# Column maxima spread by a product with the repeated column as weights; the engines of the vector steps chosen anew

## The chip, the core and the metric

The kernel runs on one core of one Trainium2 chip. A core has five engines with a queue each: TensorE (PE in the profile; its weight loads are PEld), VectorE (DVE), ScalarE (ACT), GpSimd (POOL) and SyncE (SP), which here issues every DMA. Each engine works through its own queue in order; an instruction whose input is not ready holds back all that is queued behind it. Engines wait for each other by semaphores. The metric is device microseconds (us) of one execution, lower is better.

## What is computed

One step of a hybrid attention encoder, for 1024 prompt rows with 16 meta rows ahead of them, and for 32 sample rows that attend to a cache of 272 rows:

```python
h = rmsnorm(x) * g
dq, dk, dv, fq, fk, fv, fl, gate = split(h @ w_in)      # 1024 x 4104
# 4 differential heads: two softmax maps each, subtracted
ad = softmax(q1 k1' - alibi) - lam * softmax(q2 k2' - alibi);  od = rmsnorm(ad @ dv) * subln_g * 0.2
# 8 forgetting heads: softmax with a bias from cumulative log-sigmoid gates
of = softmax(fq fk' + F_q - F_k) @ fv
y = rmsnorm(x + (concat(od, of) * silu(gate)) @ w_out) * final_norm_g
# the outputs: y, and the new rows of k, v and log f
```

All inputs and outputs are float32. To reach that accuracy with 16-bit products, each operand is split into a high and a low half (`hi = fp16(s*x)`, `lo = fp16(s*x - hi)`), and each product is made of three.

## The kernel before

Nothing in the code is in the order in which the engines run it. Functions describe tasks (`add(engine, cost, function, priority, deps, buffers taken, buffers used)`), and `Graph.order` simulates the engines with the costs given there (ns) and writes out the order: whenever an engine is idle in that simulation, the ready task with the lowest priority number gets it, if its buffers are free. The instructions are then issued in that order, so that a task with a wrong cost shifts what follows on its engine.

The main parts are these.
- `x_tasks` (lines 512 to 603): nine tiles of x are normalised and split into `hT`, the transposed input. Three tiles are transposed by PE, six by DMA. `XO` is the order of the tiles, `XG` the engine that multiplies by g ("d" DVE, "p" POOL), for the tiles that go by DMA.
- `w_tasks` (from line 654): a block of 128 columns of w_in is loaded, ACT sums the absolute values of each row (L668), `scale_tasks` turns the row sums into one scale for the whole block, and the block is split into hi and lo. The two halves are made by ACT and DVE (L687, L689), by POOL and DVE (`W_POOL`, L683), or by POOL, ACT and POOL (`W_FULL`, L674, L676, L678).
- `spread_task` (L615 to L627) brings a column of 128 values, one per partition, to all partitions: POOL makes a diagonal matrix of it (L623), PE multiplies it by a matrix of ones (L627), DVE takes the maximum over the row (L640 in `scale_tasks`, L799 in `v_tasks`). It is called 51 times: for each of the 32 blocks of w_in, the forget weights, the 8 blocks of v, w_out, and 9 tiles of the output.
- `proj_tasks`: the 32 projections (L869), their transposes and, for the gates, the chain exp, ln, exp on ACT, one product on POOL or DVE (`GATE_POOL`, L973), and two on DVE (L977, L978), which frees the accumulator.
- `unit_tasks`: 128 rows against their keys (block i has 144 + 128 i keys). Scores on PE (L1273), bias and minimum on DVE (L1287), exp on ACT (L1293), reciprocal on DVE (L1297 to L1301). For pairs 0 to 3 (differential) the second map is scaled on POOL (L1305), combined on DVE (L1317), split by ACT (L1322) and by POOL or DVE (`DIFF_POOL`, L1328). For pairs 4 to 7 (forgetting) the split is ACT and DVE (L1336, L1344), POOL and DVE (`FOX_POOL`, L1339, L1344), or POOL scale, ACT copy, POOL subtraction (`FOX_FULL`, L1350, L1355, L1361). A DMA transposes the result, and PE multiplies by v (L1385 to L1392).
- `out_tasks`: w_out is loaded, summed (L1681), scaled and split (`WO_FULL`: POOL, ACT, POOL at L1701 to L1705; `WO_POOL`: POOL L1712 and DVE L1716; else ACT L1714 and DVE L1716) into `hT`, which must be free by then. Nine output tiles: load, product with the gate (L1751), sum (L1765), spread, split (L1768, L1770), 48 products each (L1798), final norm.
- A warm-up of 24 float32 products of the identity (L1856) runs at the start.

Of the kernel before, what the change touches and what calls it, by code (L numbers as in the profile page):

```python
# [59 lines left out]
WO_POOL = (4, 7)  # L60
W_FULL = {"v": (1, 2, 4, 5, 7), "k": (0,), "q": (6,)}
FOX_FULL = (2, 3, 6)
AHEAD = 400.0
# [4 lines left out]
WARM = 24  # L68

# [193 lines left out]
def tile_hymba(  # L263
# [17 lines left out]
             "Q0": 2, "Q1": 2, "Q2": 2, "kq": 2, "diag": 2, "ge": 2, "G": 2, "kr": 1, "vr": 1, "vs": 1, "ksh": 1, "ksl": 1, "sP": 1,  # L281
# [78 lines left out]
    onesb = T([128, 128], BF16, "onesb")  # L360
# [28 lines left out]
    def consts():  # L389
# [4 lines left out]
        def f2():  # L394
# [12 lines left out]
            pool.tensor_copy(out=identb, in_=ident)  # L407
# [207 lines left out]
    def spread_task(col_, prio, deps):  # L615


        dh, th = Hold("diag"), Hold("tr")
        loc = {}

        def fd():
            loc["d"] = T([128, 128], BF16, "diag", RINGS["diag"])
            pool.tensor_scalar(out=loc["d"], in0=ident, scalar1=col_, scalar2=1.0, op0=ALU.mult, op1=ALU.mult)  # L623

        def f():
            loc["t"] = PSUM("tr")[:, 0:128]
            mm(loc["t"], onesb, loc["d"], start=True, stop=True)  # L627
        td = add("pool", 370 + PORT_P, fd, prio, list(deps) + [cn["id"]], [dh])
        return loc, th, add("pe", 60, f, prio, [td, cn["one"]], [th], [dh])

    def scale_tasks(parts, prio, deps, outs):


        m, sc = stat(), stat()
        if parts.shape[-1] > 1:
            deps = [add("dve", 150, lambda: dve.tensor_reduce(out=m, in_=parts, axis=AX.X, op=ALU.max), prio, deps)]
        loc, th, t1 = spread_task(m if parts.shape[-1] > 1 else parts, prio, deps)
# [13 lines left out]
    def w_tasks(key, prio):  # L651
# [6 lines left out]
        a, u = stat(), stat()  # L658
# [115 lines left out]
    def v_tasks(p, prio):  # L774
# [10 lines left out]
        a, b, mx, sc, u = (stat() for _ in range(5))  # L785
# [236 lines left out]
    def forget_tasks(prio):  # L1022
# [7 lines left out]
        wa, wu = stat(), stat()  # L1030
# [213 lines left out]
    def unit_tasks(p, hd, gg, prio, bias, av):  # L1244
# [5 lines left out]
        for bi in range(2):  # L1250
# [6 lines left out]
            for m in maps:  # L1257
# [38 lines left out]
                def fq(r=r, rk=rk, sm=sm, m=m):  # L1296
# [3 lines left out]
                    elif m == 0:  # L1300
                        dve.tensor_scalar(out=rk, in0=r, scalar1=lam3[1], scalar2=None, op0=ALU.mult)  # L1301
                t = add("dve", 300 + 0.4 * PORT, fq, prio + 0.3, [te, cn["lam"]])
                if p < 4 and m == 1:
                    def fp(ph=ph, nk=nk, r=r):
                        pool.tensor_scalar(out=A(ph, nk), in0=A(ph, nk), scalar1=r, scalar2=lam3[2],  # L1305
                                           op0=ALU.mult, op1=ALU.mult)
                    t = add("pool", c_ts(nk), fp, prio + 0.3, [t], [], [ph])
# [5 lines left out]
            on_pool = i in (DIFF_POOL if p < 4 else FOX_POOL)  # L1313
# [17 lines left out]
            else:  # L1331
# [15 lines left out]
                full = i in FOX_FULL  # L1347
                if full:
                    def fp(ph=P[m], nk=nk, r=rec[m][1]):
                        pool.tensor_scalar(out=A(ph, nk), in0=A(ph, nk), scalar1=r, scalar2=2.0 ** 15, op0=ALU.mult,  # L1350
                                           op1=ALU.mult)
# [11 lines left out]
                    t = add("pool", c_ts(nk), fp, prio + 0.2, [t], [], [P[m]])  # L1363
# [268 lines left out]
    def out_tasks(prio, early_q):  # L1632
# [88 lines left out]
        for t, (c0, n, j) in enumerate([(1024, 32, 8)] + [(128 * j, 128, j) for j in range(8)]):  # L1721
# [33 lines left out]
            a, u = stat(), stat()  # L1755
# [186 lines left out]
```

## Time and profile before

| | us |
|---|---|
| median of 3 runs | 774.92 |
| lowest, highest | 774.81, 775.51 |
| the profiled execution | 774.65 |
| its span, first to last instruction | 772.7 |
| mean granted TensorE clock (share of full) | 0.946 |
| busy: PE, DVE, ACT, POOL | 675.7, 601.3, 506.1, 394.4 |
| instructions | 14780 |

The profiled execution took 1.95 us more than its span, and 0.27 us less than the median. Busy time of PE is the union of its products' records; products overlap each other in time, so the row of one product is longer than its share. A row of the trace gives start and length of an instruction, or of several merged ones (x8), in us; a line number stands for the line of the kernel that issued it; `out<-in` are the names of tiles.

### The profile page before, as it was taken

Reading aid. Unit: us, or ns where it says so; the run is one execution under the profiler, and the core shown is the slowest. Engines: PE = TensorE matmul, PEld = TensorE weight load, DVE = VectorE, ACT = ScalarE, POOL = GpSimd, SP = SyncE. Lnnn points to the kernel's source line nnn. Section 1 sums busy time; section 2 is a strip of 40 time slices with the busy share of each in tenths; the row PEclk is TensorE's granted clock in tenths of the full one; section 3 lists DMA queues with packets and bytes.
Section 4 is the critical chain, followed back from the end, with each engine's and each line's share of the span. In section 5 each row is a group of like instructions: output and inputs, shape, how many; then the busy total and the mean of one; then the engine's idle time right before and its main releaser. Section 6 shows DMA issues by size and latency. Waiting matters only on the chain. (4 is left out here: it accounts for less than half of the span.)

```text
span 772.7 us, 14780 instructions
## 1 busy us (share of the span) xinstructions
PE 675.7 (87%) x4967; PEld 450.5 (58%) x4967; DVE 601.3 (78%) x1631; ACT 506.1 (66%) x1156; POOL 394.4 (51%) x542
## 2 busy tenths in 40 slices
PE   5379787998999799899799989898999984599996
PEld 5256455666666566576576667666756653234443
DVE  5975888877888588888878987886887888847643
ACT  5654666576677496687777688777679787434332
POOL 0556562586577477876748375562642455510000
PEclk8579999999999899999999999999999997599998
DMA  8376543667453565567577996795599788948411
GB/s 235 79 168 116 120 109 51 93 131 113 71 134 89 109 139 111 119 146 135 133 112 151 162 208 147 152 190 153 113 223 221 164 195 231 262 136 244 145 55 55
DMA packets 236444, 110.48 MB, mean 143 GB/s; under 512 B 150112, under 2 KB 228264, under 8 KB 236368
## 3 DMA queue, kind: packets, MB, share of 16 engines
q1 hardware_dynamic: 236368, 109.54, 65.6%
q8 instruction: 39, 0.64, 0.3%
q14 instruction: 37, 0.30, 0.1%
HBM read 46.39 MB, written 21.87 MB: 88 GB/s over the span
## 5 line engine op out<-in xcount | busy, mean ns | idle before, releaser
L869 PE MATMUL pj<-hT,W 128*128 128x416 f16 (+4 forms) x1776 | 292.1, 318 | 9.0 <-DVE ge L978 6.5
L869 PEld LDWEIGHTS <-W 128*128 128x128 f16 x1776 | 175.7, 101 | 104.1 <-issue 20.7
L1287 DVE CUSTOM_DVE_ANT_0 arena<-sc,G,stats 128x400 f32<-128x400 f32 (+9 forms) x224 | 128.4, 590 | 22.7 <-PE sc L1273 12.3
L1293 ACT ACTIVATE arena<-arena,stats 128x528 f32<-128x528 f32 (+7 forms) x128 | 99.8, 780 | 26.5 <-DVE stats L1287 25.5
L1798 PE MATMUL pj<-hT,W 128*128 128x512 f16 (+4 forms) x440 | 95.8, 373 | 1.9 <-DVE arena L1812 0.8
L869 PE MATMUL pj<-hT,Wg 128*128 128x416 f16 (+2 forms) x576 | 93.9, 315 | 2.9 <-DVE ge L978 2.9
L1273 PE MATMUL sc<-k,q 128*128 128x400 f16 (+9 forms) x448 | 89.0, 313 | 5.4 <-DMA k<-k 2.9
L623 POOL TENSOR_SCALAR diag<-ident,stats 128x128 bf16<-128x128 f32 x51 | 26.6, 522 | 102.7 <-ACT W L1765 52.4
L869 PEld LDWEIGHTS <-Wg 128*128 128x128 f16 x576 | 55.6, 98 | 32.2 <-issue 5.6
L1798 PEld LDWEIGHTS <-W 128*128 128x128 f16 (+2 forms) x440 | 41.7, 99 | 54.1 <-issue 9.4
L1328 POOL TENSOR_TENSOR arena<-arena 128x16 f16<-128x16 f32 (+7 forms) x56 | 48.1, 879 | 33.9 <-ACT arena L1322 32.3
L1389 PE MATMUL av<-arena,vn 128*128 128x128 f16 x288 | 41.0, 226 | 18.2 <-DMA arena<-arena 18.0
L1273 PEld LDWEIGHTS <-q 128*128 128x128 f16 x448 | 39.7, 100 | 23.8 <-DMA k<-k 4.0
L1361 POOL TENSOR_TENSOR arena<-arena 128x16 f16<-128x16 f32 (+3 forms) x48 | 40.9, 872 | 18.7 <-ACT arena L1355 18.6
L1344 DVE SCALAR_TENSOR_TENSOR arena<-arena,stats 128x128 f16<-128x128 f32 (+4 forms) x80 | 48.1, 647 | 2.7 <-ACT arena L1336 2.5
L888 ACT ACTIVATE zT<-pj 128x416 f32<-128x416 f32 (+4 forms) x50 | 22.6, 451 | 37.0 <-PE pj L869 32.9
L1350 POOL TENSOR_SCALAR arena<-arena,stats 128x400 f32<-128x400 f32 (+2 forms) x24 | 22.1, 921 | 44.9 <-DVE stats L1297 28.5
L1390 PE MATMUL av<-arena,vn 128*128 128x128 f16 x288 | 41.1, 226 | 0.0
L1390 PEld LDWEIGHTS <-vn 128*128 128x128 f16 x288 | 29.2, 101 | 18.3 <-issue 16.2
L1389 PEld LDWEIGHTS <-vn 128*128 128x128 f16 x288 | 29.1, 101 | 16.2 <-issue 9.0
L1305 POOL TENSOR_SCALAR arena<-arena,stats 128x144 f32<-128x144 f32 (+7 forms) x32 | 29.6, 928 | 11.0 <-DVE stats L1297 7.4
L1297 DVE RECIPROCAL stats<-stats 128x1 f32<-128x1 f32 x128 | 19.7, 156 | 19.9 <-ACT arena L1293 18.9
(306 smaller groups left out, 1496.7 us busy)
## 6 DMA issues: line engine op xcount, KB each, us to landing
raw<-in_w_in_dram SPq DMA_DIRECT2D x32, 512.0 KB, 9.6
arena<-in_x_prompt_dram SPq DMA_DIRECT2D x16, 512.0 KB, 3.6
k<-k SPq DMA_DIRECT2D x24, 268.0 KB, 3.5
G<-G_t SPq DMA_DIRECT2D x8, 520.0 KB, 4.4
mix_s<-mx SPq DMA_DIRECT2D x32, 128.0 KB, 2.8
arena<-mix_s SPq DMA_DIRECT2D x8, 512.0 KB, 5.4
arena<-gate_s SPq DMA_DIRECT2D x8, 512.0 KB, 7.1
out_dram<-arena SPq DMA_DIRECT2D x16, 256.0 KB, 2.3
```

The lines of the kernel that those rows point to most:

```text
L623: pool.tensor_scalar(out=loc["d"], in0=ident, scalar1=col_, scalar2=1.0, op0=ALU.mult, op1=ALU.mult)
L869: mm(out, (W["hi"], W["hi"], W["lo"])[w][:, k, :], (hTh, hTl, hTh)[w][:, k, c0:c1], start=i == 0, stop=i == 23)
L1273: mm(s[:, :b - a], q, K[p]["t"][:, m, x, a:b], start=x == 0, stop=x == 1 and not mask)
L1287: dve.tensor_tensor_reduce(out=A(ph, nk)[:, a:b], in0=loc["s"][:, :b - a], in1=bl["t"][:, o + a:o + b], scale=Q[p]["tau"], scalar=3e38 if ...
L1293: te = add("act", c_act(nk) + 125, lambda ph=ph, nk=nk, mn=mn, sm=sm: act.activation(out=A(ph, nk), in_=A(ph, nk), func=AF.Exp, scale=-1.0 ...
L1305: pool.tensor_scalar(out=A(ph, nk), in0=A(ph, nk), scalar1=r, scalar2=lam3[2], op0=ALU.mult, op1=ALU.mult)
L1328: (pool if on_pool else dve).tensor_tensor(out=A16(w, o, o + b - a), in0=x[:, a:b], in1=A16(w, h, h + b - a), op=ALU.subtract)
L1344: dve.scalar_tensor_tensor(out=A16(w, o, o + b - a), in0=x[:, a:b], scalar=rk, in1=A16(w, h, h + b - a), op0=ALU.mult, op1=ALU.subtract)
L1361: pool.tensor_tensor(out=A16(w, o, o + b - a), in0=x[:, a:b], in1=A16(w, h, h + b - a), op=ALU.subtract)
L1389: mm(out, vn[:, j, 128 * hd:128 * hd + 128], hi, start=j == 0, stop=False)
L1390: mm(out, vn[:, j, 128 * hd:128 * hd + 128], lw, start=False, stop=False)
L1798: mm(d, a, b, start=k == 0 and i == 0, stop=k == 7 and i == len(ops) - 1)
```

## The change

1. `spread_task` has no diagonal: the column itself, kept in bf16 and repeated 128 times by its access pattern, is the stationary operand of the product, and the identity the moving one. POOL's L623 goes, with its ring of two buffers and the matrix of ones. The sums go to bf16 columns (`stat16`). The bf16 identity is made with the first constants.
2. The second scalar of POOL's scalings in `unit_tasks` becomes a constant: DVE now makes `r * lam3[2]` for the second map, too (one more 128x1 instruction per unit of pairs 0 to 3).
3. The scaling of a `FOX_FULL` unit goes to ACT for blocks 0, 2, 4 and 7 (`F1_ACT`). Pair 7 has its own lists of engines (`LAST_POOL`, `LAST_FULL`).
4. 40 tasks of four float32 products of the identity (`KEEP`), planned at 460 ns each, with the last priority of all: PE gets one whenever the plan has nothing else for it.
5. The constants that choose engines, order and priorities are set anew.

```diff
-G_AT = (130, 140, 289, 261, 189, 300, 359, 331)
+G_AT = (130, 140, 300, 261, 189, 240, 359, 331)
-WO_PRIO = 260
+WO_PRIO = 400
-WO_FULL = (2, 4)
-DIFF_POOL = (0, 1, 3, 4, 5, 6, 7)
-FOX_POOL = (2, 5)
-GATE_POOL = (0, 1, 3, 4, 5, 6, 7)
-K_POOL = (1, 2, 3, 4, 6)
-XG = "ppddpddpd"
+WO_FULL = (0, 3, 4)
+DIFF_POOL = (0, 1, 2, 3, 4, 5, 6, 7)
+FOX_POOL = (0, 1, 2, 6, 7)
+GATE_POOL = (1, 3, 4, 7)
+K_POOL = (0, 1, 2, 3, 4, 5, 6)
+XG = "pddddddpd"
-XO = (8, 0, 1, 2, 5, 4, 3, 6, 7)
+XO = (0, 8, 1, 2, 3, 4, 5, 7, 6)
-FIRST = {"v": -892, "k": -864, "q": -870}
-W_POOL = {"k": (1, 2, 3, 4, 6), "g": (0, 3, 4, 7), "v": (1, 5, 6), "q": (0, 5, 6)}
-WO_POOL = (4, 7)
-W_FULL = {"v": (1, 2, 4, 5, 7), "k": (0,), "q": (6,)}
-FOX_FULL = (2, 3, 6)
-AHEAD = 400.0
+FIRST = {"v": -892, "k": -864, "q": -867}
+W_POOL = {"k": (0, 1, 2, 3, 4, 6), "g": (3, 4, 5), "v": (1, 2, 6), "q": (0, 5, 6)}
+WO_POOL = (1, 2, 7)
+W_FULL = {"v": (2, 4, 5, 7), "k": (0,), "q": (6,)}
+FOX_FULL = (2, 3, 5, 6, 7)
+AHEAD = 200.0
+KEEP = 40
+P1_ACT = ()
+F1_ACT = (0, 2, 4, 7)
+LAST_POOL = (2, 3, 5, 7)
+LAST_FULL = (5, 6, 7)
...
-        dh, th = Hold("diag"), Hold("tr")
+        th = Hold("tr")
         loc = {}
-
-        def fd():
-            loc["d"] = T([128, 128], BF16, "diag", RINGS["diag"])
-            pool.tensor_scalar(out=loc["d"], in0=ident, scalar1=col_, scalar2=1.0, op0=ALU.mult, op1=ALU.mult)
 
         def f():
             loc["t"] = PSUM("tr")[:, 0:128]
-            mm(loc["t"], onesb, loc["d"], start=True, stop=True)
-        td = add("pool", 370 + PORT_P, fd, prio, list(deps) + [cn["id"]], [dh])
-        return loc, th, add("pe", 60, f, prio, [td, cn["one"]], [th], [dh])
+            mm(loc["t"], col_.broadcast_to([128, 128]), identb, start=True, stop=True)
+        return loc, th, add("pe", 60, f, prio, list(deps) + [cn["id"]], [th])
...
-            on_pool = i in (DIFF_POOL if p < 4 else FOX_POOL)
+            on_pool = i in (DIFF_POOL if p < 4 else FOX_POOL if p < 7 else LAST_POOL)
...
-                full = i in FOX_FULL
+                full = i in (FOX_FULL if p < 7 else LAST_FULL)
...
-                    t = add("pool", c_ts(nk), fp, prio + 0.2, [t], [], [P[m]])
+                    t = add("act" if i in F1_ACT else "pool", c_act(nk) if i in F1_ACT else c_ts(nk), fp, prio + 0.2, [t], [], [P[m]])
...
     def f1():
         make_identity(nc, ident)
+        pool.tensor_copy(out=identb, in_=ident)
...
-    cn["one"] = add("dve", 150, lambda: dve.memset(onesb, 1.0), -1000)
...
+    for i in range(KEEP):
+        kh = Hold("av")
+
+        def fk():
+            t = PSUM("av")
+            for i in range(4):
+                mm(t[:, 0:128], ident, ident, start=True, stop=True)
+        add("pe", 460, fk, 500000, [cn["id"]], [kh])
```

## Rows read from the trace of the kernel before

**Rows 1.** The page, part 1: busy time, share of the span and instructions by engine.
```profile
PE 675.7 (87%) x4967; PEld 450.5 (58%) x4967; DVE 601.3 (78%) x1631; ACT 506.1 (66%) x1156; POOL 394.4 (51%) x542
```
**Rows 2.** Stretches: length, busy PE, PEld, DVE, ACT, POOL, granted clock, DMA share, GB/s.
```profile
14.00:45.00 31.00, 13.95 (x84) 10.94 (x84) 28.67 (x50) 19.58 (x37) 13.52 (x7) 0.56 0.56 148
45.00:49.00 4.00, 0.00 (x0) 0.00 (x0) 2.25 (x5) 3.46 (x4) 0.25 (x1) 0.89 0.46 103
49.00:55.00 6.00, 5.28 (x34) 4.43 (x34) 4.09 (x12) 3.25 (x11) 4.99 (x2) 0.50 0.62 125
...
90.00:400.00 310.00, 282.12 (x2136) 193.89 (x2135) 253.31 (x725) 216.31 (x527) 201.23 (x272) 0.97 0.58 113
400.00:638.00 238.00, 223.36 (x1862) 156.44 (x1860) 199.06 (x604) 183.54 (x419) 126.00 (x185) 1.00 0.82 172
638.00:672.00 34.00, 14.96 (x124) 10.50 (x122) 29.24 (x45) 21.24 (x32) 20.66 (x13) 0.66 0.99 238
```
**Rows 3.** What PE waited for between 60 and 640: us in total, times, longest.
```profile
PE pj L869 <- DVE ge L978: 9.4, 8, 4.3
PE av L1385 <- DMA arena<-arena: 8.8, 6, 3.9
PE av L1389 <- DMA arena<-arena: 8.6, 6, 3.2
```
**Rows 4.** Groups by shape, whole span: busy us, mean ns, then idle before them.
```profile
L623 POOL TENSOR_SCALAR diag<-ident,stats 128x128 bf16<-128x128 f32 x51 | 26.6, 522 | 102.7 <-ACT W L1765 52.4 <-ACT W L668 35.4 <-ACT Wg L668 7.5
...
L1344 DVE SCALAR_TENSOR_TENSOR arena<-arena,stats 128x1024 f16<-128x1024 f32 x8 | 13.3, 1660 | 0.5 <-ACT arena L1336 0.4
L1361 POOL TENSOR_TENSOR arena<-arena 128x896 f16<-128x896 f32 x8 | 16.2, 2023 | 11.8 <-ACT arena L1355 11.8
L973 POOL TENSOR_TENSOR ge<-ge,gr 128x256 f32<-128x256 f32 (+2 forms) x21 | 20.5, 976 | 16.1 <-ACT gr L969 13.2 <-DVE stats L1559 2.6
L973 DVE TENSOR_TENSOR ge<-ge,gr 128x256 f32<-128x256 f32 (+2 forms) x3 | 1.6, 523 | 0.8 <-ACT gr L969 0.8
L1301 DVE TENSOR_SCALAR stats<-stats 128x1 f32<-128x1 f32 x32 | 6.9, 214 | 1.1
```
**Rows 5.** PE in order of time at the start: start, length, what.
```profile
7.83 1.95 PE L1856 MATMUL pj<-ident 128*128 128x128 f32 x16
...
21.77 2.92 PE L869 MATMUL pj<-hT,W 128*128 128x144 f16 x23 [1.49 <-DVE hT L576]
...
50.05 4.79 PE L869 MATMUL pj<-hT,W 128*128 128x256 f16 x32
...
65.08 2.78 PE L869 MATMUL pj<-hT,W 128*128 128x256 f16 x24
```
**Rows 6.** POOL and DVE at the start, in order of time.
```profile
23.64 3.96 POOL L586 TENSOR_TENSOR arena<-arena,G 128x1024 f32<-128x1024 f32 x1
...
16.80 2.19 DVE L558 SCALAR_TENSOR_TENSOR arena<-arena,stats,G 128x512 f32<-128x512 f32 x2
...
25.37 4.21 DVE L558 SCALAR_TENSOR_TENSOR arena<-arena,stats,G 128x512 f32<-128x512 f32 x2
```
**Rows 7.** ACT, POOL and DVE between 656 and 668, in order of time.
```profile
659.74 1.04 ACT L1765 ACTIVATE W<-arena 128x1024 bf16<-128x1024 f32 x1
...
656.64 2.15 POOL L1712 TENSOR_SCALAR hT<-raw,stats 128x1024 f16<-128x1024 f32 x1
658.76 3.08 POOL L1705 TENSOR_TENSOR hT<-W,hT 128x1024 f16<-128x1024 f32 x1
...
664.89 1.34 POOL L623 TENSOR_SCALAR diag<-ident,stats 128x128 bf16<-128x128 f32 x1
...
662.85 4.45 DVE L1716 SCALAR_TENSOR_TENSOR hT<-raw,stats,hT 128x1024 f16<-128x1024 f32 x2
```
**Rows 8.** The same operations elsewhere: groups by shape, whole span.
```profile
L1770 DVE SCALAR_TENSOR_TENSOR W<-arena,stats,W 128x1024 f16<-128x1024 f32 x8 | 10.3, 1282 | 2.7 <-ACT W L1768 2.7
L678 POOL TENSOR_TENSOR W<-raw,W 128x1024 f16<-128x1024 f32 x7 | 15.8, 2254 | 5.6 <-ACT W L676 5.4
```

More of the change, by code (lines that the diff above doesn't have):

```diff
@@ L68 @@
 WARM = 24
+KEEP = 40
[3 more added lines that the diff above has]
+LAST_FULL = (5, 6, 7)
+G_STEP = 0.1
 class Hold:
@@ L379, in stat, with stat16 @@
         return stats[:n, c:c + 1]
+    ctx.enter_context(nc.allow_low_precision(reason="they only choose a scale"))
+    def stat16():
+        col16[0] += 1
+        return stats16[:, col16[0] - 1:col16[0]]
     def A16(h, c0, c1):
@@ L784, in v_tasks @@
         v["nh"] = nh
-        a, b, mx, sc, u = (stat() for _ in range(5))
+        mx, sc, u = (stat() for _ in range(3))
+        a, b = stat16(), stat16()
         U[p] = u
@@ L1299, in fq @@
                         dve.tensor_scalar(out=rk, in0=r, scalar1=2.0 ** 15, scalar2=None, op0=ALU.mult)
-                    elif m == 0:
-                        dve.tensor_scalar(out=rk, in0=r, scalar1=lam3[1], scalar2=None, op0=ALU.mult)
+                    else:
+                        dve.tensor_scalar(out=rk, in0=r, scalar1=lam3[1 + m], scalar2=None, op0=ALU.mult)
                 t = add("dve", 300 + 0.4 * PORT, fq, prio + 0.3, [te, cn["lam"]])
                 if p < 4 and m == 1:
[L1304 to L1307, printed above, removed]
+                    if i in P1_ACT:
+                        t = add("act", c_act(nk), lambda ph=ph, nk=nk, rk=rk: act.activation(
+                            out=A(ph, nk), in_=A(ph, nk), func=AF.Identity, scale=rk), prio + 0.3, [t], [], [ph])
+                    else:
+                        t = add("pool", c_ts(nk), lambda ph=ph, nk=nk, rk=rk: pool.tensor_scalar(
+                            out=A(ph, nk), in0=A(ph, nk), scalar1=rk, scalar2=1.0, op0=ALU.mult, op1=ALU.mult),
+                            prio + 0.3, [t], [], [ph])
                 rec[m] = (t, r, rk)
@@ L1346, in unit_tasks, with fp @@
                 t = rec[m][0]
-                full = i in FOX_FULL
+                full = i in (FOX_FULL if p < 7 else LAST_FULL)
                 if full:
-                    def fp(ph=P[m], nk=nk, r=rec[m][1]):
-                        pool.tensor_scalar(out=A(ph, nk), in0=A(ph, nk), scalar1=r, scalar2=2.0 ** 15, op0=ALU.mult,
-                                           op1=ALU.mult)
+                    def fp(ph=P[m], nk=nk, rk=rec[m][2], on_act=i in F1_ACT):
+                        if on_act:
+                            act.activation(out=A(ph, nk), in_=A(ph, nk), func=AF.Identity, scale=rk)
+                        else:
+                            pool.tensor_scalar(out=A(ph, nk), in0=A(ph, nk), scalar1=rk, scalar2=1.0, op0=ALU.mult,
+                                               op1=ALU.mult)
                     def fh(nb=nb, w=w, ph=P[m], nk=nk):
```

20 lines of the change are left out of this document (10 added, 10 removed).

## The prediction

> **What bounds the kernel now.** I read the page's busy shares first. PE is busy for 675.7 of 772.7 us, DVE for 601.3, ACT and POOL for less [rows 1]. So an engine that is relieved gives nothing by itself; what can be won is PE's idle time, 97 us, and products that ran at half clock. The table of stretches says where these lie [rows 2]. In the first one, 14 to 45 us, PE does 13.95 us of work at a granted clock of 0.56 (near the lower of the two levels, 1.2 and 2.4 GHz), while DVE is busy for 28.67 of 31 us: the x tiles bound this stretch, by DVE. From 55 us on PE is close to full: 27.9 us idle in 90 to 400, 14.6 us in 400 to 638. Between 638 and 672 it does 15 us of work in 34, at 0.66. Behind that, the output products run back to back, and the last few us are a chain that the change does not touch. So three places count: the start, the waits of the long middle, and the passage from attention to the output projection. For the middle I read PE's waits: 9.4 us for DVE's L978, which frees an accumulator behind the gates' chain, and 17.4 us for the DMA that transposes the attention weights, thus for the end of the split of a unit [rows 3]. Two thirds of the idle time of the middle are these.
>
> **The spread.** 51 POOL instructions of 0.52 us go, 26.6 us [rows 4]. POOL idles elsewhere, so this is worth something only where PE or DVE waits for L623. In the middle, blocks of weights are loaded ahead, and none of PE's large waits there names it: zero; without the blocks loaded ahead it would be 0.5 us per block. One chain counts: the first output tile. Its row sum ends at 660.8, POOL reaches the diagonal at 664.89 behind L1712 and L1705, and takes 1.34 us [rows 7]. Without it, PE has the column 5 us earlier, but DVE, which takes the maximum next, is in L1716 until 667.3 [rows 7]. So between 0 and 5 us; the order is made anew and the maximum can go between two L1716, so I take 3, nearer to the 5. The product itself has the same shapes as before. Repeating a column as weights is not in this trace; a slower weight load is hidden behind products or costs at most one cold product each, and I take zero.
>
> **DVE and POOL in the middle.** Block 7 of pairs 4 to 6 leaves DVE: six units at 1.66 us, 10.0 us [rows 4]. Block 5, three quarters as wide, 1.25 us by the same row, gives 7.5. Pair 7 moves the same two blocks, but blocks 2 and 3 return to DVE: about 3 us off. Against that, DVE gets nine gate products of 0.52 us (4.7) and 32 tiny L1301 (6.9) [rows 4]. With blocks 2 of pairs 0 to 3 and seven K subtractions going to POOL (some 0.5 us each by L973's row, 5 us), DVE loses 14 us. POOL loses 26.6 (diagonals) and 8.8 (nine gate products of 0.98), and gains six subtractions of 2.3 us (2.02 us at 896 columns, scaled to 1024) and six of 1.7, some 24 us, some 4 us for pair 7, and some 11 us for K and blocks 2 [rows 4]. So POOL stays about where it is, and DVE falls by 2%. PE does not wait for DVE's total, but for two chains. The gates' chain: nine of the 21 POOL products go, each leg shorter by 0.45 us; in proportion 9/21 of 9.4 us, at most 4.0. I take 2.5. The transposes: a unit of block 7 now ends with a POOL subtraction that is some 0.5 us longer than DVE's, 16 such units (blocks 5 and 7), up to 8 us of delay in chains that PE waits for; or half of the 17.4 us go, since DVE reaches the reciprocals and minima earlier. I take 1 us of gain; the two ends are 8 lost and 8.7 won. Middle: minus 3.5.
>
> **The start.** Three things. First, g times the fifth x tile goes from POOL to DVE. POOL took 3.96 us for it, and DVE's two L558 beside it took 4.21 us instead of 2.19 [rows 6]. DVE gets about 1.2 to 1.7 us of work and loses 2.0 us of slowness, and POOL's leg of 4 us goes: I take 1.5 us of gain, between 0 and 4. Second, KEEP holds the clock. Of 21.8 us idle between 14 and 55 us [rows 2] the plan would fill a good part. What is there to win: 23 products of 144 columns took 2.92 us and 32 of 256 took 4.79, where 24 of 256 later take 2.78 [rows 5], so 1.5 and 3.7 at full clock: 2.5 us together. The bound is half of all work at the low clock, 7.0 and 2.6 us [rows 2], 9.6. On the path, nearer to the two rows: 3 us. Third, the price of KEEP. The plan charges 460 ns for four products. In the trace 8 such products (two records each, 16 records) take 1.95 us [rows 5], 0.98 us for four; 40 tasks are 39 us where the plan sees 18.4, and the real idle time is 21.8. The excess, 17 us, is PE running late. What it does to the end depends on who waits for PE there: the DMA-transposed tiles don't, three tiles and three spreads do, and PE idles 4 us from 45 on, which swallows some. Between 0 and 17 us; I take 3, near the lower end, since DVE, with 28.67 us of 31, is what the stretch waits for. Start: minus 1.5.
>
> **The passage.** Besides the spread, w_out's split moves: three full weights on POOL instead of two, three high halves on POOL instead of one, five L1716 on DVE instead of six. While both engines were full there, DVE's L1716 took 2.2 us where the same operation alone takes 1.28, and POOL's L1705 3.08 us where it takes 2.25 [rows 7, 8]. POOL gets one subtraction and three scalings more, 3.08 + 3 x 2.15 = 9.5 us at those rates [rows 7]; DVE loses 2.2 us. PE consumes the eight weights in order, so that it can begin on the first ones while the last are split, if the first output tile is ready; today that tile is late (above). That it starts earlier takes off 6 us at most, the later end of the split adds 9.5 us less what PE can do meanwhile; I leave the passage at the 3 us of the spread. Its range is minus 6 to plus 9.5.
>
> **Sum.** -1.5 - 3.5 - 3 = -8.0 us on the profiled execution's 774.65, so 766.65, and with the 0.27 us to the median 766.9. I say 767.
>
> **A rule that speaks against the change.** The rows just read show DVE and POOL slowing each other: L558 4.21 against 2.19, L1716 2.2 against 1.28. The Trainium skill, SBUF — State Buffer, "Who interferes with whom", says more: a DVE instruction with two SBUF inputs and a POOL instruction that reads SBUF exclude each other for the whole instruction. By that rule moving a split from DVE to POOL frees nothing, as the two engines' times add up, and the passage would be longer by the third rival below; the doubled L558 agrees with it.
>
> **The rivals.**
> - KEEP overruns (slower). The 40 tasks stand in front of real work and all 17.2 us of excess count, less the 3 us of clock: start +12.7 instead of -1.5 (g's 1.5 included); with the other two as forecast +6.2, 781. It decides from about 22 tasks (21.8 us of idle time at 0.98) ahead of 55 us. For it: a product of float32 is plainly longer than the plan's 115 ns [rows 5]. Against it: DVE bounds the stretch, and a warm PE gives some back.
> - Most of the waits go (faster). Start -4, middle -8, passage -6: 757. For it: DVE leaves the chains that PE waits for. Against it: each wait that goes uncovers the next engine, ACT and POOL.
> - POOL becomes the bound of the passage (slower). POOL's 9.5 us come at the end of the split, and PE stands for them: +9.5 there instead of -3; with the rest at -5, +4.5, 779. It decides where POOL's share of w_out ends after DVE's. For it: DVE is busy for 29.24 of 34 us there, POOL for 20.66 [rows 2], and they slow each other. Against it: the order can put POOL's weights last.
> - No difference. The spread hides behind DVE, and the waits of the middle only move: 774 to 776.5.
>
> **How the numbers follow.** Differences under 0.2%, 1.5 us, are what a measurement of this kernel can't tell from none. Forecast (760 to 773) 0.52, most waits go (752 to 760) 0.14, KEEP overruns (777 to 789) 0.16, POOL in the passage (776.5 to 784) 0.10, no difference 0.08. Faster: 0.52 + 0.14 = 0.66; same 0.08; slower 0.26. For 8 in 10 I leave out the half of the fast rival below 756 (0.07) and the upper parts of the slow ones above 782 (0.11): 756 to 782. Within the forecast alone 760 to 773.
>
> **What would show it.** Spread: no L623, and the first output tile's L1768 less than 4 us behind the end of its L1765 (now at least 6.5: from 660.8 to DVE's 667.3). Clock: stretches from 14 to 55 near 1.0. KEEP: its rows; harmless if PE's first long run of L869 still begins by 50 us, harmful if 55 or later. Middle: PE's idle time from 90 to 638 at 39 instead of 42.5, waits for L978 under 7. Passage: PE's 15 us of work from 638 within some 31 us instead of 34. I am wrong if the start of PE's long run moves by more than 5 us, if POOL's last L1705 ends later than 20 us behind the scale of w_out, or if POOL's subtractions make the waits for transposes grow above 20 us.

## The result, and the profile after

| | before | after |
|---|---|---|
| median, us (lowest, highest, runs) | 775.21 (774.81, 777.13, 4) | 796.77 (794.01, 798.08, 4) |
| profiled execution, its span | 774.65, 772.7 | 798.08, 796.3 |
| mean granted clock | 0.946 | 0.965 |

The changed kernel is slower: ratio 1.028, interval 1.024 to 1.032, where 767 us had been forecast. Line numbers moved: L869 is now L878, L627 L635, L640 L648, L736 L744, L978 L987, L1344 L1356, L1361 L1376, L1385 and L1389 L1400 and L1404, L1705 L1720, L1716 L1731, L1751 L1766, L1765 L1780, L1768 L1783, L1798 L1813; KEEP is L1880.

After, the stretches cut as before (length, busy PE, PEld, DVE, ACT, POOL, granted clock, DMA share, GB/s):

```profile
14.00:45.00 31.00, 30.94 (x286) 30.53 (x285) 19.38 (x42) 16.00 (x35) 3.25 (x2) 1.00 0.33 84
45.00:49.00 4.00, 4.00 (x39) 4.00 (x38) 2.10 (x1) 3.14 (x7) 0.00 (x0) 1.00 0.01 3
49.00:55.00 6.00, 6.00 (x58) 5.51 (x56) 3.81 (x10) 2.13 (x2) 2.08 (x1) 1.00 1.01 268
90.00:400.00 310.00, 284.76 (x2174) 193.60 (x2173) 262.21 (x769) 218.90 (x536) 197.16 (x275) 0.97 0.56 115
400.00:638.00 238.00, 212.15 (x1715) 146.31 (x1713) 172.82 (x517) 170.83 (x378) 125.65 (x179) 0.98 0.79 156
```

Against [rows 2] PE is full from 14 to 55 us, at full clock, and from 14 to 49 the other engines do less: DVE 19.38 us instead of 28.67 from 14 to 45, POOL 3.25 instead of 13.52, and from 45 to 49 the DMA moves 3 GB/s. From 90 to 638 PE idles 51.1 us instead of 42.5. What fills PE at the start is KEEP. Its group by shape (count, busy us, mean ns, idle before) and PE in order of time (start, length):

```profile
L1880 PE MATMUL av<-ident 128*128 128x128 f32 x320 | 37.4, 276 | 0.1
```

```profile
9.71 5.52 PE L1880 MATMUL av<-ident 128*128 128x128 f32 x48
...
19.57 11.83 PE L1880 MATMUL av<-ident 128*128 128x128 f32 x104
31.33 1.08 PE L577 MATMUL av<-ident,arena 48*128 48x48 f32 x8
...
40.83 9.99 PE L1880 MATMUL av<-ident 128*128 128x128 f32 x88
...
60.45 4.79 PE L878 MATMUL pj<-hT,W 128*128 128x256 f16 x32
```

The 40 tasks take 37.4 us where the plan has 18.4. All 40 run before 51 us. The transposes of the 48-row tile (L577) stand among them, at 31.33, and the run of 32 products of 256 columns begins at 60.45 instead of 50.05 [rows 5].

What PE waited for between 60 and 640 after (us in total, times, longest), to be held against [rows 3]:

```profile
PE tr L744 <- ACT zT L897: 13.7, 7, 4.7
PE pj L878 <- DVE ge L987: 9.0, 7, 3.7
...
PE av L1404 <- DMA arena<-arena: 4.7, 6, 1.2
...
PE av L1400 <- DMA arena<-arena: 1.9, 1, 1.9
```

The waits for the transposed weights did fall, from 17.4 to 6.6 us. In their place PE waits for ACT's copies (L744), 13.7 us, where the same wait (L736) was 2.9 before.

### The profile page after: what moved, and what is told of

Read it like the earlier page. It is cut to its first block, busy times and chain, and to the rows that moved or that the text cites. A ratio compares the mean times of both kernels' runs of the same rounds, so it can differ in the third digit from the quotient of the medians.

```text
span 796.3 us, 15418 instructions
## 1 busy us (share of the span) xinstructions
PE 712.2 (89%) x5287; PEld 481.4 (60%) x5287; DVE 598.1 (75%) x1633; ACT 510.6 (64%) x1152; POOL 400.2 (50%) x536
## 5 line engine op out<-in xcount | busy, mean ns | idle before, releaser
L878 PE MATMUL pj<-hT,W 128*128 128x416 f16 (+4 forms) x1776 | 292.2, 317 | 6.1 <-DVE ge L987 5.2
L878 PEld LDWEIGHTS <-W 128*128 128x128 f16 x1776 | 173.3, 100 | 93.5 <-issue 12.8
L1296 DVE CUSTOM_DVE_ANT_0 arena<-sc,G,stats 128x400 f32<-128x400 f32 (+8 forms) x224 | 128.6, 591 | 24.9 <-PE sc L1282 13.6
L1302 ACT ACTIVATE arena<-arena,stats 128x144 f32<-128x144 f32 (+7 forms) x128 | 99.8, 780 | 29.8 <-DVE stats L1296 28.2
L878 PE MATMUL pj<-hT,Wg 128*128 128x416 f16 (+2 forms) x576 | 97.0, 318 | 8.1 <-DVE ge L987 4.8
L1813 PE MATMUL pj<-hT,W 128*128 128x512 f16 (+4 forms) x440 | 97.1, 376 | 1.3 <-DVE W L1785 1.3
L1282 PE MATMUL sc<-k,q 128*128 128x400 f16 (+8 forms) x448 | 89.8, 312 | 8.9 <-DVE stats L1296 6.4
L1376 POOL TENSOR_TENSOR arena<-arena 128x768 f16<-128x768 f32 (+4 forms) x72 | 71.5, 1018 | 43.1 <-ACT arena L1370 37.4
L878 PEld LDWEIGHTS <-Wg 128*128 128x128 f16 x576 | 55.6, 99 | 38.0 <-issue 10.6
L1813 PEld LDWEIGHTS <-W 128*128 128x128 f16 (+2 forms) x440 | 42.2, 100 | 53.4 <-issue 10.9
L1340 POOL TENSOR_TENSOR arena<-arena 128x128 f16<-128x128 f32 (+7 forms) x64 | 54.7, 876 | 31.5 <-ACT arena L1334 31.4
L1404 PE MATMUL av<-arena,vn 128*128 128x128 f16 x288 | 40.7, 226 | 10.3 <-DMA arena<-arena 5.2
L648 DVE TENSOR_REDUCE stats<-tr 128x1 f32<-128x128 f32 x43 | 12.4, 288 | 43.4 <-PE tr L635 42.9
L744 PE MATMUL tr<-ident,zT 128*128 128x128 f32 (+2 forms) x160 | 26.9, 281 | 13.9 <-ACT zT L897 13.7
L1880 PE MATMUL av<-ident 128*128 128x128 f32 x320 | 37.4, 276 | 0.1
L1832 ACT ACTIVATE arena<-arena 128x512 bf16<-128x512 f32 (+3 forms) x19 | 11.5, 604 | 39.5 <-DVE arena L1827 39.5
L1880 PEld LDWEIGHTS av<-ident 128*128 128x128 f32 x320 | 36.4, 192 | 0.3 <-PE av L1880 0.2
L1404 PEld LDWEIGHTS <-vn 128*128 128x128 f16 x288 | 29.2, 102 | 10.7 <-ACT arena L1370 5.1
```

The costliest lines, as they stand in the source:

```text
L744: pe.transpose(t[:n, s, :], loc["zT"][:, c - c0:c - c0 + n], ident)
L878: mm(out, (W["hi"], W["hi"], W["lo"])[w][:, k, :], (hTh, hTl, hTh)[w][:, k, c0:c1], start=i == 0, stop=i == 23)
L1282: mm(s[:, :b - a], q, K[p]["t"][:, m, x, a:b], start=x == 0, stop=x == 1 and not mask)
L1296: dve.tensor_tensor_reduce(out=A(ph, nk)[:, a:b], in0=loc["s"][:, :b - a], in1=bl["t"][:, o + a:o + b], scale=Q[p]["tau"], scalar=3e38 if ...
L1302: te = add("act", c_act(nk) + 125, lambda ph=ph, nk=nk, mn=mn, sm=sm: act.activation(out=A(ph, nk), in_=A(ph, nk), func=AF.Exp, scale=-1.0 ...
L1340: (pool if on_pool else dve).tensor_tensor(out=A16(w, o, o + b - a), in0=x[:, a:b], in1=A16(w, h, h + b - a), op=ALU.subtract)
```

## Experiment 1: what KEEP costs

Three kernels keep the changed kernel's plan, and so its written order, and alter only what a KEEP task issues; a fourth plans without KEEP.

e1 has bf16 fillers:

```diff
-                mm(t[:, 0:128], ident, ident, start=True, stop=True)
+                mm(t[:, 0:128], identb, identb, start=True, stop=True)
```

> The changed kernel with its 40 filler tasks (four products each) made of bf16 identities instead of float32 ones; same places in the order, same planned cost of 460 ns. Theory A (the float32 fillers take twice what the plan charges, so PE runs late): the fillers' 37.6 us of PE shrink to some 10, PE's run of 32 products of 256 columns begins near 50 us as before instead of 60.4, and the time falls by 10 to 12 us, to 785 to 787; to 775 if the further 11 us behind the start are only the late start carried on. Rival B (the new choice of engines costs the 11 us of the middle): the start recovers and the time stays at 784 to 788. Rival C (the new order of the x tiles makes the start late, the fillers sit in idle time): 795 or more.

e2 has the tasks in its plan, but they issue nothing:

```diff
         def fk():
-            t = PSUM("av")
-            for i in range(4):
-                mm(t[:, 0:128], ident, ident, start=True, stop=True)
+            pass
```

> The changed kernel planned with its 40 filler tasks, but none of their products issued; the order of all else is the same. Theory A: as the bf16 fillers, 785 to 787, plus what the low clock costs at the start: 2.5 to 6 us more than with bf16 fillers if a warm PE matters there, 0 if not. Rival C: 795 or more.

g3 issues two float32 products in a task instead of four:

```diff
-            for i in range(4):
+            for i in range(2):
                 mm(t[:, 0:128], ident, ident, start=True, stop=True)
```

> The changed kernel with two float32 products in a KEEP task instead of four: the plan and the order are the same, and a task takes some 0.48 us, near the planned 460 ns. Theory (the excess over the planned price is what costs): 780 to 784, as with bf16 fillers (782.5) and with empty tasks (782.1), and the first run of 32 products of 256 columns begins at 45 to 48 us. Rival (fillers cost by being there, in proportion): half of the 14 us, 789.

e3 is planned without the tasks:

```diff
-KEEP = 40
+KEEP = 0
```

> The changed kernel with KEEP = 0, so that the plan is made without fillers (the order differs from the start on). Theory A: start as before the change, 782 to 788 if the middle keeps its 11 us, 770 to 776 if it does not. Rival C: 793 or more.

| | median, us | ratio to before (interval) |
|---|---|---|
| changed kernel, 4 products a task | 796.77 | 1.0282 (1.0244 to 1.0320) |
| e1, bf16 | 782.50 | 1.0103 (1.0031 to 1.0175) |
| e2, nothing | 782.13 | 1.0102 (1.0046 to 1.0158) |
| g3, two products | 785.19 | 1.0127 (1.0083 to 1.0171) |
| e3, planned without | 781.64 | 1.0081 (1.0050 to 1.0112) |

With the same order, leaving the fillers out gives back 1.0282 - 1.0102 = 1.8%, 14 us. Two products a task (0.49 us, near the planned 0.46) cost 0.25%, inside the intervals. The 40 shorter tasks of g3 take 19.5 us where the plan has 18.4. So the excess over the plan is what costs, not the presence of fillers. Fillers of about the planned length and the clock that they hold together gain nothing that can be measured; no run has the clock without the fillers. The stretch from 14 to 45 us of e2 (columns as above), and PE's runs of 256 columns in order of time (the bracket is the wait):

```profile
14.00:45.00 31.00, 13.91 (x84) 10.76 (x84) 27.00 (x51) 22.62 (x43) 8.47 (x5) 0.57 0.54 145
```

```profile
35.81 6.79 PE L878 MATMUL pj<-hT,W 128*128 128x256 f16 x40
45.67 0.44 PE L744 MATMUL tr<-ident,zT 128*128 128x128 f32 x2 [3.08 <-ACT zT L897]
45.95 2.54 PE L878 MATMUL pj<-hT,W 128*128 128x256 f16 x32
```

The same of g3, with its fillers as a group (count, busy us, mean ns, idle before):

```profile
14.00:45.00 31.00, 23.55 (x211) 21.80 (x209) 26.54 (x53) 22.58 (x43) 7.24 (x4) 0.98 0.50 134
```

```profile
L1880 PE MATMUL av<-ident 128*128 128x128 f32 x160 | 19.5, 277 | 0.1
```

```profile
37.05 4.53 PE L878 MATMUL pj<-hT,W 128*128 128x256 f16 x40
46.93 0.69 PE L744 MATMUL tr<-ident,zT 128*128 128x128 f32 x2 [5.36 <-ACT zT L897]
47.42 4.03 PE L878 MATMUL pj<-hT,W 128*128 128x256 f16 x32
```

Clock 0.57 in one and 0.98 in the other, DVE about as busy in both, and the run of 32 begins at 45.95 and 47.42. The 40 products ahead of it are 2.3 us shorter in g3; they begin 1.2 us later, behind fillers, and what is left goes into a longer wait for ACT (5.36 us instead of 3.08). In the changed kernel the run of 32 begins at 60.45, 14.5 us behind e2. PE has the same 4967 other products in the same order in both; paired one by one from there on, those of the changed kernel come 11 to 20 us later, and the output products by 14.8 us to the end. A run of 24 of these, after:

```profile
694.88 8.01 PE L1813 MATMUL pj<-hT,W 128*128 128x512 f16 x24
```

and in e2:

```profile
680.10 8.04 PE L1813 MATMUL pj<-hT,W 128*128 128x512 f16 x24
```

So the delay at the start goes through to the end.

How the delay passes through DVE, which bounded this stretch before, is told by the waits of ACT, then of DVE, between 14 and 55 us in the changed kernel (us in total, times, longest):

```profile
ACT hT L582 <- PE sc L577: 8.5, 2, 7.2
ACT hT L582 <- PE av L577: 7.6, 1, 7.6
```

```profile
DVE hT L588 <- ACT hT L582: 10.3, 2, 5.5
DVE stats L648 <- PE tr L635: 6.0, 2, 3.2
```

PE's transposes stand behind fillers in PE's queue (those of L577 begin at 31.33, in e2 at 19.36), ACT copies late, and DVE, whose next instruction in its queue is the low half of that tile, idles 10.3 us; behind it are the next tiles. e2 has neither of these DVE waits among its largest.

The fillers were tried in the kernel before, too:

```diff
+    for i in range(40):
+        kh = Hold("av")
...
+        add("pe", 460, fk, 500000, [cn["id"]], [kh])
```

> The kernel before with the same 40 float32 filler tasks added and nothing else changed. Theory A: its start is as late as that of the changed kernel, PE's run of 32 products begins near 60 us, and the time rises by 9 to 14 us, to 784 to 789. Rival C: within 3 us of the kernel before.

810.26 us, ratio 1.046 (1.041 to 1.052), some 36 us. Its run of 256 columns begins at 59.37, only 9.3 us late; the rest is lost behind that. But here the plan is made anew with 40 more tasks, so this run mixes the fillers with another order. That led to the next question.

## Experiment 2: code, engines, order, and a change of nothing

Without KEEP the changed kernel is still 6 to 8 us slower than before. f1 to f3 have the new code and no KEEP: f1 with all old constants, f2 with the new engine sets alone, f3 with the new order constants alone; e3 above has both. f4 and g2 are the kernel before with one planned cost altered (370 to 400 in f4, to 340 in g2), g4 is e3 with one altered. They issue the same instructions as their base, in another order. The edit of f4, and that of g4:

```diff
-        td = add("pool", 370 + PORT_P, fd, prio, list(deps) + [cn["id"]], [dh])
+        td = add("pool", 400 + PORT_P, fd, prio, list(deps) + [cn["id"]], [dh])
```

```diff
-        return loc, th, add("pe", 60, f, prio, list(deps) + [cn["id"]], [th])
+        return loc, th, add("pe", 90, f, prio, list(deps) + [cn["id"]], [th])
```

> The new code (spread without the diagonal, second scalar folded into DVE's L1301) with all of the old constants and no KEEP. Without KEEP and with the new constants the kernel took 781.6 us, before 773.5 beside it: 8 us are to be placed. Theory E (the new choice of engines loses them): this one is as before or up to 3 us faster, 770.5 to 774.5, since the engines are the old ones. Theory O (the new order constants lose them): the same 770.5 to 774.5. Rival S (no single choice: the written order is made anew from the planned costs, and another order of the same work lands some us higher): anywhere from 773 to 783, without a cause that can be named by the edit. Rival P (the spread itself costs: PE waits in its own queue for ACT's row sum where POOL's diagonal waited for it before): 778 to 782, and PE's waits ahead of the spread's product, which lie at 18.6 us of idle time in the kernel before, grow by 5 us or more.

> As f1, with the new choice of engines (gates, K, weights, units, w_out, g of x), the order constants old, no KEEP. Theory E: 780 to 783, the whole loss is here, and PE's progress falls behind from 400 us on as it did with all new constants. Theory O: as f1 or up to 4 us faster, 768 to 774.5. Rival S: 773 to 785, not the sum of f1 and the engines' part.

> As f1, with the new order constants (G_AT, WO_PRIO, XO, FIRST, AHEAD), the engines old, no KEEP. Theory E: 771 to 775. Theory O: 780 to 783. Rival S: 773 to 785; and over f1, f2, f3 and the kernel with both the four effects don't add up (f2 + f3 - f1 differs from 781.6 by over 4 us).

> The kernel before with one planned cost changed: the task of the diagonal is planned 30 ns longer. Every instruction is the same; the written order on all engines differs from about 90 us on. Theories E and O, P: 772 to 775.5, as before (773.5), since no work is moved. Rival S: over 3 us from before, above all upwards, 777 to 785.

> The kernel before with the diagonal's task planned 30 ns shorter: the same instructions in another written order. Theory S: over 3 us from before, above all upwards, 777 to 795, as with 30 ns longer (786.8). Rival (the longer price was at fault there, as POOL's diagonals were put too late): 770 to 775.

> The changed kernel without KEEP (781.6 us) with one planned cost changed: the spread's product is planned at 90 ns instead of 60. The same instructions in another order. Theory S: over 3 us from 781.6, upwards or downwards, 770 to 800. Rival (the scatter belongs to the kernel before alone, the new plan is as good as it gets): 780 to 783.

| | median, us | ratio to before (interval) |
|---|---|---|
| f1, new code alone | 792.47 | 1.0210 (1.0151 to 1.0269) |
| f2, and new engines | 803.65 | 1.0357 (1.0299 to 1.0416) |
| f3, and new order constants | 781.81 | 1.0081 (1.0052 to 1.0111) |
| e3, both | 781.64 | 1.0081 (1.0050 to 1.0112) |
| f4, diagonal planned 30 ns longer | 786.78 | 1.0157 (1.0078 to 1.0236) |
| g2, 30 ns shorter | 807.04 | 1.0414 (1.0370 to 1.0458) |
| g4, e3 with the spread planned 30 ns longer | 784.65 | 1.0135 (1.0096 to 1.0174) |

The effects don't add up (f2 + f3 - f1 would be 793 us, e3 is 781.6), and 30 ns in one planned cost, in either direction, cost the kernel before 1.6% and 4.1%. Theories E and O fall: neither "the engines" nor "the constants" loses the 8 us as a quantity of its own. Another written order alone moves the time of the kernel before by as much and more. Without KEEP the changed kernel moved less: g4 is 0.5%, 4 us, above e3, and the two intervals overlap. All three altered plans came out slower than their base; why was not tried. f4's page, part 1, and its second stretch of the middle (columns as above):

```profile
PE 680.2 (87%) x4967; PEld 451.6 (58%) x4967; DVE 600.5 (77%) x1631; ACT 506.9 (65%) x1156; POOL 394.5 (50%) x542
```

```profile
400.00:638.00 238.00, 217.92 (x1764) 151.99 (x1763) 185.43 (x559) 175.49 (x401) 115.35 (x174) 0.98 0.84 167
```

g2's page, and both of its stretches:

```profile
PE 684.3 (85%) x4967; PEld 453.2 (56%) x4967; DVE 605.9 (75%) x1631; ACT 506.7 (63%) x1156; POOL 389.3 (48%) x542
```

```profile
90.00:400.00 310.00, 275.31 (x2056) 187.92 (x2055) 245.58 (x697) 207.89 (x506) 195.74 (x267) 0.96 0.52 109
400.00:638.00 238.00, 214.36 (x1751) 149.96 (x1749) 182.43 (x556) 169.68 (x391) 110.94 (x172) 0.99 0.82 159
```

PE's busy time falls from 223.36 [rows 2] to 217.92 and 214.36 in the second stretch, in g2 by another 6.8 us in the first, and all four engines do less in the second stretch. Over the whole span PE idles 103.0 us in f4 (783.2 less 680.2) and 124.4 in g2 (808.7 less 684.3), where it was 97.0; its busy time grows by 4.5 and 8.6, at a mean clock of 0.942 and 0.937 instead of 0.946. So most of the loss is idle time. Which chains it is, was not followed. Rival P (PE stands in its queue ahead of a spread whose row sum isn't there) is seen in f1, where the largest of PE's waits between 55 and 720 us is

```profile
PE tr L635 <- ACT W L1780: 11.3, 2, 8.1
```

but the next experiment shows that this belongs to f1's order and not to the spread.

## Experiment 3: one term at a time, in the old order

To try a part without a new plan, the kernel before keeps its tasks, planned costs and so its order; only what a task issues is changed, at the same place. A task that is moved to another engine so stands at a place that was planned for the old one: these runs tell what a term is worth in this order, not what it would be worth in a plan made for it.

g1 issues no diagonal, and the sums go to bf16 columns:

```diff
-            loc["d"] = T([128, 128], BF16, "diag", RINGS["diag"])
-            pool.tensor_scalar(out=loc["d"], in0=ident, scalar1=col_, scalar2=1.0, op0=ALU.mult, op1=ALU.mult)
+            pass
...
-            mm(loc["t"], onesb, loc["d"], start=True, stop=True)
+            mm(loc["t"], col_.broadcast_to([128, 128]), identb, start=True, stop=True)
```

> The kernel before with its written order kept on every engine: the task of the diagonal stays in the plan at its planned cost but issues nothing, and the spread's product takes the repeated bf16 column as weights and the identity as moving operand. So the spread is tried alone, without a new order. The prediction gave it 3 us in the passage (0 to 5) and nothing elsewhere: 770 to 773.5 beside a kernel before of 773.5 to 775.6, PE's wait ahead of the spread (18.6 us of idle time before) down by some us. Rival P (the repeated column costs as weights, or PE now waits for ACT): 777 or more. Theory S says nothing against a gain here, since the order is the same; by it, f1's 792.5 was the order's, so this one is 15 us or more below f1.

h1 issues the gates' products of pairs 0, 5 and 6 on DVE:

```diff
-                    (pool if p in GATE_POOL else dve).tensor_tensor(out=e, in0=e, in1=r, op=ALU.mult)
+                    (pool if p in (1, 3, 4, 7) else dve).tensor_tensor(out=e, in0=e, in1=r, op=ALU.mult)
```

> The kernel before in its own written order; only the nine gate products of pairs 0, 5 and 6 are issued on DVE instead of POOL, at the same places. The prediction's term: -2.5 us, at most -4, by shorter legs ahead of L978; PE's waits for L978 fall from 9.4 to under 7. Rival (DVE's queue is the later one, so the leg only moves): 0 to +3, waits for L978 as before or longer.

h2 issues g times the fifth tile on DVE:

```diff
-                dve if e == "dve" else pool).tensor_tensor(
+                dve if e == "dve" or o == 4 else pool).tensor_tensor(
```

> The kernel before in its own written order; only g times the fifth x tile is issued on DVE instead of POOL. The prediction's term: -1.5 us (0 to -4), and the run of 32 products of 256 columns begins 1 to 4 us before 50.05. Rival (DVE bounds the start with 28.67 of 31 us, so 1.2 us more on it is 1.2 us more): 0 to +1.5.

h3 splits blocks 5 and 7 of pairs 4 to 6 as the changed kernel does:

```diff
+                if i in (5, 7) and p < 7:
...
+                        if i == 7:
+                            act.activation(out=x, in_=x, func=AF.Identity, scale=rk)
+                        else:
+                            pool.tensor_scalar(out=x, in0=x, scalar1=r, scalar2=2.0 ** 15, op0=ALU.mult, op1=ALU.mult)
+                        act.activation(out=A16(w, 0, nb), in_=x[:, 16:nk], func=AF.Copy)
...
+                            pool.tensor_tensor(out=A16(w, o, o + b - a), in0=x[:, a:b], in1=A16(w, h, h + b - a),
+                                               op=ALU.subtract)
```

> The kernel before in its own written order; the splits of blocks 5 and 7 of pairs 4 to 6 are issued as in the changed kernel (scale on POOL for 5, on ACT for 7, copy on ACT, subtraction on POOL; 24 instructions of DVE go), at the places of the old ones. The prediction's term for all such moves: -1 us (-8.7 to +8). Rival (POOL's subtraction ends later, and PE waits for the transposes): +3 to +8, PE's waits ahead of the transposed weights from 26.8 to over 32 us.

h4 has all these edits.

> The kernel before in its own written order with the spread of g1 and the three moves of h1 to h3 together. By the prediction's terms, added to g1's measured -4.3: -9.3 us, 766 beside 775. If the terms hold only where nothing else comes next: -3 to -5, 770 to 772, as g1 alone. Rival (the moves without a plan made for them cost more than they give): slower than g1 by over 3 us.

Differences in us are the ratio times before's 775.7:

| | median, us | ratio (interval) | difference, us | predicted |
|---|---|---|---|---|
| g1, spread | 770.26 | 0.9944 (0.9922 to 0.9965) | -4.3 | -3 |
| h2, g of a tile | 773.14 | 0.9965 (0.9940 to 0.9989) | -2.7 | -1.5 |
| h1, gates' products | 776.76 | 1.0020 (0.9994 to 1.0046) | +1.6 | -2.5 |
| h3, splits | 782.20 | 1.0076 (1.0048 to 1.0103) | +5.9 | -1 |
| h4, all four | 776.52 | 1.0006 (0.9984 to 1.0029) | +0.5 | -8 |

In one order the terms do add up: -4.3 - 2.7 + 1.6 + 5.9 = +0.5, and h4 has +0.5. h4 is 0.6%, 4.8 us, slower than g1, as the rival recorded for it had it (over 3 us: moves without a plan made for them cost more than they give). The runs don't tell this rival from terms that are wrong in any plan: with plans made for them, the new engines cost 1.5% in f2 against f1 and nothing in e3 against f3. And f1, the same spread in a new order (besides 32 tiny DVE instructions), is 2.7%, 21 us, above g1.

**The splits.** PE's waits in h3 between 60 and 640, and h3's second stretch:

```profile
PE pj L869 <- DVE ge L978: 12.5, 8, 4.2
PE av L1400 <- DMA arena<-arena: 9.0, 4, 3.9
PE tr L736 <- ACT zT L888: 5.9, 3, 3.6
...
PE av L1404 <- DMA arena<-arena: 2.8, 3, 1.2
```

```profile
400.00:638.00 238.00, 219.58 (x1832) 154.39 (x1830) 178.84 (x569) 191.11 (x431) 143.12 (x202) 1.00 0.84 169
```

The waits for transposes fall to 11.8 us from 17.4. My rival, which counted them from a base of 26.8, had them over 32; over the whole span, too, they fall (L1400 and L1404 9.0 + 12.7 us, L1385 and L1389 before 8.8 + 22.5). What grows is behind ACT: its busy time there goes from 183.54 [rows 2] to 191.11, the copies that PE waits for from 2.9 to 5.9, the gates' chain (exp, ln and exp in it are ACT's) from 9.4 to 12.5. It is the pattern of the changed kernel: fewer waits for transposes, more for ACT. This is read from the waits of one execution and not tried by itself. It also leaves part of the 5.9 us open, since PE's idle time from 90 to 638 grows by 2.6 us only (45.1 instead of 42.5).

**The gates.** In h1 PE waits for L978 for longer, not shorter:

```profile
PE pj L869 <- DVE ge L978: 10.8, 9, 4.2
```

Paired gate by gate, the nine moved products take 4.7 us on DVE where they took 8.3 on POOL, but they begin 11.7 us in total behind the end of ACT's L969 instead of 5.8. From there to the end of L978 the nine chains take 34.3 us instead of 32.7.

**The tile.** In h2 DVE's two L558 are fast (2.17 us, not the 4.21 of [rows 6]), and PE's run begins at 47.90, not at 50.05:

```profile
24.74 2.17 DVE L558 SCALAR_TENSOR_TENSOR arena<-arena,stats,G 128x512 f32<-128x512 f32 x2
```

```profile
47.90 2.54 PE L869 MATMUL pj<-hT,W 128*128 128x256 f16 x32
```

**The spread.** g1's gain is not where I put it. At the start PE's wait ahead of its third spread falls, from 7.14 us for POOL's diagonal to 4.80 for ACT (PE in order of time, before and then g1, with the run of 32 in g1; the bracket is the wait):

```profile
38.39 0.27 PE L627 MATMUL tr<-diag,onesb 128*128 128x128 bf16 x1 [7.14 <-POOL diag L623]
```

```profile
35.88 0.29 PE L632 MATMUL tr<-identb,stats 128*128 128x128 bf16 x1 [4.80 <-ACT W L674]
...
49.90 3.63 PE L876 MATMUL pj<-hT,W 128*128 128x256 f16 x32
```

That spread comes 2.5 us earlier, but the run of 32 only 0.15 (50.05 before [rows 5]), as PE waits for ACT's copy ahead of it. Paired one by one, g1's products come 1.3 us earlier at 84 us, 2.5 in the median from 100 to 638, and 3.1 at 638. So the gain is there long before the passage; only its first part is traced to a wait. In the passage, DVE's maximum before, then PE and DVE in g1:

```profile
667.22 0.28 DVE L640 TENSOR_REDUCE stats<-tr 128x1 f32<-128x128 f32 x1
```

```profile
658.81 0.29 PE L632 MATMUL tr<-identb,stats 128*128 128x128 bf16 x1 [1.25 <-ACT W L1772]
```

```profile
661.75 2.47 DVE L1723 SCALAR_TENSOR_TENSOR hT<-raw,stats,hT 128x1024 f16<-128x1024 f32 x2
664.14 0.28 DVE L646 TENSOR_REDUCE stats<-tr 128x1 f32<-128x128 f32 x1
```

The column is spread at 658.8, but DVE takes its maximum at 664.14, behind the last half of w_out's L1716 (here L1723). That is 3.1 us earlier than before, as much as g1 was ahead at 638: in the passage itself next to nothing is won.

## Experiment 4: the wait behind the wait

i1 joins the two terms that won. i2 adds a move of three tasks in the finished order: DVE's maximum of the first output tile goes ahead of the last three L1716. In the diff, `ts` and `t3` are the tasks of that tile's scale and low half, `late` the low halves of w_out's last three weights.

```diff
     seq = g.order()
+    ts, t3 = min(cn["tiles"], key=lambda x: seq.index(x[0]))
+    late = cn["ws"][5:]
+    for t in late:
+        seq.remove(t)
+    seq.insert(seq.index(ts) + 1, late[0])
+    seq[seq.index(t3) + 1:seq.index(t3) + 1] = late[1:]
```

> The kernel before in its own written order with the two moves that were faster by themselves: the spread without the diagonal (-4.3 us measured) and g times the fifth x tile on DVE (-2.7). If they add up: 768 to 769 beside 775.5, ratio 0.991. Rival (both take the same wait at the start away): -4.5, 771.

> As i1, with one more change of the written order by hand: on DVE the maximum and the scale of the first output tile stand ahead of the last three of w_out's L1716, one of which follows the scale and two the low half of that tile. In g1 the column was spread at 658.8 and DVE came to it at 664.1, behind three L1716. Theory (DVE's queue hides the passage's gain): the first output product begins 3 to 4 us earlier than in i1, the time is 3 us less, 765 to 766. Rival (the products then wait for the low halves of the last weights, or the wait moves to the next tile): within 1 us of i1.

i1: 769.77 us, ratio 0.9938 (0.9910 to 0.9965). i2: 767.19 us, 0.9885 (0.9854 to 0.9916). i1's -4.8 us lies between the full sum and no sum, and its interval (-7.0 to -2.7) holds both. i2 is faster again, by 2.6 us by the medians and 4.1 by the ratios (the two intervals just overlap), and beats both kernels. PE's first output products (start, length; the bracket is the wait) in i1:

```profile
667.03 1.03 PE L1805 MATMUL pj<-hT,W 128*128 128x512 f16 x2 [4.89 <-ACT W L1775]
```

and in i2:

```profile
661.32 1.03 PE L1807 MATMUL pj<-hT,W 128*128 128x512 f16 x2 [1.31 <-ACT W L1776]
```

The wait falls from 4.89 to 1.31 us. Of the 5.7 us between the two starts, some 2 were there before the moved tasks, from one execution to the other: paired one by one, i2's products come 2.1 us earlier up to the first output products and 5.0 after them, so that 2.9 are won there. So the passage does hold the 3 us of the prediction, once DVE is free when the column is.

## Why the prediction was wrong, point by point

- **The price of KEEP** is the term that failed most. The prediction worked out an excess of 17 us over PE's idle time (39 - 21.8; with the measured 37.4 it is 15.6, and over the plan's 18.4 it is 19) and took 3 of it "since DVE, with 28.67 us of 31, is what the stretch waits for". It cost 14. DVE was not a cover: three tiles go through PE, and DVE's queue stands while PE is behind. The rival named this mechanism with 17.2 us and a chance of 0.16. Its own signs came true: the run begins at 60.45, past 55, with all 40 tasks ahead of it. Its time of 777 to 789 was still too low, since the 6 to 8 us that are left without KEEP (below) were in none of the rivals.
- **The clock**, -3: from 14 to 55 it was at full speed, as forecast, and with fillers of about the planned length it gave nothing measurable (e2 against g3): what the shorter products gained went into a later start and a longer wait for ACT.
- **The g tile**, -1.5 within 0 to -4: -2.7, by the mechanism told.
- **The spread**, -3 within 0 to -5: -4.3, but ahead of the passage and not in it; its first part is at the start (PE's wait of 7.1 us for a diagonal, which I had passed over in PE's waits). There the step "the maximum can go between two L1716" was not given by the order; i2 made it so by hand. The number came near by luck: the place was wrong.
- **The gates**, -2.5: +1.6 (interval -0.5 to +3.6). I scaled POOL's leg and left out that DVE comes to the product later, which in h1 takes more than the shorter product gives (5.9 us against 3.6 over the nine).
- **The splits**, -1 within -8.7 to +8: +5.9. I weighed POOL against DVE and the transposes, and did not count ACT at all, though block 7's scaling and block 5's copy go to ACT (1.15 and 0.83 us each in the trace after). In both h3 and the changed kernel the waits for transposes fell, and waits for ACT's copies grew; that ACT is the cause is read from the waits, not shown.
- **The order** was missing from the sum. The prediction treated a new plan as neutral. A plan altered by 30 ns in one cost moved the kernel before by +11 and +31 us, so the 6 to 8 us that the changed kernel without KEEP is slower are within what a new order does; they are not ascribed to any edit. Not tried singly are the moves of weights, K and w_out between the engines and the new list for pair 7.
- **What would show it**: no diagonal, and L1783 comes some 2 us behind the end of L1780 (under 4, as said). PE's idle time from 90 to 638 went to 51.1, not 39; waits for L987 stay at 9.0, not under 7. The waits for transposes went to 6.6, not above 20. The last L1720 ends 24 us behind the scale of w_out (669.8 to 693.9; before 648.9 to 664.9), over the 20 that I had named. How much of that late end is the order's and how much POOL's share was not tried, and so the rival of POOL in the passage stays open. That the two engines slow each other there, as the prediction feared, is seen: DVE's product with the gate for the 32 sample rows (L1766) took 2.33 us beside POOL's last L1720 (690.8 to 693.9), and 0.42 before. After, PE's next spread, at 694.80, waits 3.54 us for ACT's row sum of that product. DVE after, then before:

```profile
691.87 2.33 DVE L1766 TENSOR_TENSOR arena<-arena 128x256 f32<-128x256 f32 x1
```

```profile
667.91 0.42 DVE L1751 TENSOR_TENSOR arena<-arena 128x256 f32<-128x256 f32 x1
```

## To carry to other kernels

Where the order of issue comes from a plan, try an edit first inside the old order, and measure what a meaningless change of the plan does; without that, an edit can't be told from a new order. A filler, or any work planned below its true length, can be paid nearly in full (here 14 of 19 us) when another engine waits in its own queue for something behind it; an engine's busy share does not tell that it covers such a delay. When a wait is removed, look up in the trace what the next engine in the chain is doing at that moment, and move that too.

## What the runs showed of the hardware

A float32 product of 128 x 128 took 0.23 us at a granted clock of 1.00 (37.4 us for 160 in the changed kernel). In e1 160 bf16 products of the same shape took 11.5 us, 0.07 us each, partly at the lower clock (0.78 from 14 to 45 us). A product whose weights are one column repeated 128 times costs what one with a full matrix costs: 227 ns after, 232 in g1, 230 before, on average of 51 each. The group after (count, busy us, mean ns, idle before):

```profile
L635 PE MATMUL tr<-identb,stats 128*128 128x128 bf16 x51 | 11.6, 227 | 18.3 <-DVE stats L1296 7.0 <-ACT W L676 5.4 <-ACT W L1780 3.5
```

and before:

```profile
L627 PE MATMUL tr<-diag,onesb 128*128 128x128 bf16 x51 | 11.8, 230 | 18.6 <-POOL diag L623 17.5 <-DVE stats L799 1.1
```
